# Column-tiled level products and paired heads in the chunked recurrence of a two-block model

## The chip, the core and the metric

The kernel runs on one core of a Trainium2 chip. TensorE (PE) multiplies, VectorE (DVE), ScalarE (ACT) and GpSimd (POOL) work element by element, and SyncE (SP) issues the loads. The metric is device time in microseconds: 2993.26 us is the median of three runs of the kernel before (2992.8 to 2993.64).

## The reference, cut to what matters

The program computes two blocks of two layers each for 1024 tokens. The change lies in the first block, whose two layers hold a gated recurrence of 4 heads, each with 128 channels:

```python
diff = G[:, :, :, None, :] - G[:, :, None, :, :]
decay = jnp.exp(jnp.where(causal, diff, MASK_VALUE))
scores = jnp.einsum('bhtd,bhsd,bhtsd->bhts', qc, kc, decay)
o = (jnp.einsum('bhts,bhsv->bhtv', scores, vc)
     + jnp.einsum('bhtd,bhdv->bhtv', qc * jnp.exp(G), S))
```

The score of query t and key s is the product over the channels of q at t, k at s and every forget gate between the two. The output of each head is then normalised over its channels, multiplied by a gate and goes into an up projection.

## The kernel before, in words

**Stages.** The first block runs as layer 0 half 0, layer 0 half 1, layer 1 half 0 and layer 1 half 1; a half is 512 tokens, four blocks of 128 tokens side by side. Each half-layer is a list of units. A unit (`col_unit`) loads a weight slab, splits it into a high and a low part (`split_w`: the cast `wh` and the difference `wl`) and runs `unit`, 24 matmuls of 512 columns (L261 to L263; 12 in the up projections), whose rate sets the pace.

**Fibers.** Everything else is written as Python generators (fibers). Each `yield` ends a step, and after every 24 matmuls (`tick`, `TICK`) each live fiber is advanced by one step, so that its products stand between two units. `finish` runs fibers to their end at once. `Engine` keeps a running load, by which `copy` and `tt` choose between DVE, ACT and POOL. The instructions of each engine are in the order in which the framework's scheduler then puts them, and each engine works its queue in that order.

**The recurrence.** `hgrn_half` is one fiber for one head and one half. It builds the scores by doubling the distance b between neighbours. After every level the second members of the pairs of q are multiplied on DVE by the gates (L791), the first members of k on POOL (L794), in place, and the gate products `tot` are shortened. The scores of the level are the product of k and q, of which a mask lets through what belongs to that level:

- b = 1 (L741): 8 products of 64 keys with 128 columns, written to PSUM rows 0 to 63 and 64 to 127 in turn (column tiles);
- b = 2, 4, 8, 16 (`level`, L725): 4 products of 128 keys with 128 queries, and one `copy_predicated` of 128 rows by 512;
- b = 32 (L770) and b = 64 (L783): 8 products of 32 by 32 (two column tiles in turn) and 4 of 64 by 64 (one column tile).

Each of these products is in f32 and shows in the trace as two passes, two LDWEIGHTS and two MATMUL. Then come the transpose of k (L806), the states (L813), the output (L838, L842), its squares, their mean (L397 with `ones_h`), the reciprocal root (`rstd_of`: a Sqrt on ACT, then a RECIPROCAL and three SCALAR_TENSOR_TENSOR on DVE) and the last two steps: a scaling of the output by it on DVE (L851) and the product with the gate (L854).

**Order of the heads.** `head(hd)` appends three units (forget gate, query, output gate). When the third is done, `gwork` spawns the head's fiber. Units of `gates_a` stand between the heads, so before the change the four fibers start 3, 6, and 6 units apart and overlap. `bsplit` waits for all four (`finish(st["hf"])`) after the sixth `gate_h` unit and splits their results; two units and a half later `up_h` of column 0 is the first to read them. The softmax attention (L636 to L713) runs as fibers of its own beside all that; its L703 and L709 are column-tiled too.

## Time and profile before

| | |
|---|---|
| median of 3 runs | 2993.26 us |
| profiled execution, time | 2993.03 us |
| its span | 2991.1 us |
| granted TensorE clock, mean | 0.992 |
| PE, DVE, ACT, POOL busy | 98%, 56%, 49%, 37% |

PE is busy all along, and the chain of work that ended last lies on PE for 92% of the span. A row of the timeline gives the start, the length, the engine, the line, the operation and the tiles; matmuls overlap in their pipeline, so what one costs is read from the start of it to the start of the next, not from its length.

### The profile page before, as it was taken

What the parts mean: (1) busy time and instruction counts of PE and PEld (TensorE: products, weight loads), DVE (VectorE), ACT (ScalarE), POOL (GpSimd) and SP (SyncE); (2) the same over time, 40 slices, a digit from 0 to 9 for tenths busy, and PEclk for the clock granted to TensorE, in tenths of its full rate; (3) what the DMA queues carried; (4) which work ended last, traced back from release to release, by engine and by line L of the source; (5) the groups of instructions that cost most, each with busy time, mean ns of one, the idle gap of its engine ahead of it and who ended that gap; (6) DMA issues with size and microseconds to landing.
All of it is one profiled execution on the core that took longest, in us unless ns stands there. A gap on an engine that the chain in (4) does not pass through costs nothing.

```text
span 2991.1 us, 43769 instructions
## 1 busy us (share of the span) xinstructions
PE 2927.6 (98%) x16204; PEld 2431.8 (81%) x16204; DVE 1683.4 (56%) x3322; ACT 1455.9 (49%) x2946; POOL 1098.8 (37%) x1182
## 2 busy tenths in 40 slices
PE   7999999999999999999999999999999899999997
PEld 7787887888878888788888888888888788878777
DVE  6657745556556566766666533435334644454456
ACT  5765326742357433574334455335544645564553
POOL 3545433543435433545332333213332322232332
PEclk9999999999999999999999999999999999999999
DMA  3212242122521224312243222533234111111123
GB/s 129 71 64 95 88 148 85 64 71 91 170 85 68 74 80 160 106 64 78 74 152 131 99 96 95 176 102 124 99 110 165 57 38 61 38 61 43 64 99 113
DMA packets 101493, 283.47 MB, mean 95 GB/s; under 512 B 11288, under 2 KB 15512, under 8 KB 101280
## 3 DMA queue, kind: packets, MB, share of 16 engines
q1 hardware_dynamic: 100016, 279.51, 27.6%
q8 instruction: 128, 2.10, 0.3%
q10 hardware_dynamic: 1264, 1.17, 0.1%
q14 instruction: 85, 0.70, 0.1%
HBM read 259.66 MB, written 20.97 MB: 94 GB/s over the span
## 4 chain that ended last, share of the span: by engine, by line
PE 92%; DVE 3%; issue 2%; POOL 1%; ACT 1%; DMA 1%; DVEq 0%; SPq 0%; POOLq 0%; ACTq 0%
PE mm L261 21%; PE mm L262 21%; PE mm L263 21%; PE mm L305 3%; PE mm L304 3%; PE mm L303 3%; DVE hp L76 2%; PE aux L725 2%; PE aux L1500 2%; PE aux L1546 2%; PE aux L1536 2%; PE mm L275 1%; PE mm L277 1%; PE mm L276 1%; PE aux L656 1%
## 5 line engine op out<-in xcount | busy, mean ns | idle before, releaser
L261 PE MATMUL mm<-hp,wh 128*128 128x512 f32 (+1 forms) x2816 | 1117.8, 397 | 0.0
L262 PE MATMUL mm<-hp,wh 128*128 128x512 f32 (+1 forms) x2816 | 1093.4, 388 | 1.8 <-POOL hp L76 1.8
L263 PE MATMUL mm<-hp,wl 128*128 128x512 f32 (+1 forms) x2816 | 1093.2, 388 | 0.0
L76 POOL TENSOR_TENSOR wl<-raw,wh 128x512 fp32r<-128x512 f32 x367 | 493.0, 1345 | 788.5 <-ACT wh L76 677.7
L76 ACT CAST wh<-raw 128x512 fp32r<-128x512 f32 x581 | 358.5, 620 | 681.7 <-PE mm L262 467.2
L76 POOL TENSOR_TENSOR hp<-hp,hp 128x256 f32<-128x256 f32 (+3 forms) x353 | 387.6, 1105 | 672.0 <-DVE hp L76 236.3
L261 PEld LDWEIGHTS mm<-hp,wh 128*128 128x128 f32 x2816 | 530.1, 188 | 115.3 <-issue 11.5
L263 PEld LDWEIGHTS mm<-hp,wl 128*128 128x128 f32 x2816 | 529.7, 188 | 109.9 <-issue 0.2
L262 PEld LDWEIGHTS mm<-hp,wh 128*128 128x128 f32 x2816 | 530.5, 188 | 104.3 <-POOL hp L76 3.1
L76 DVE TENSOR_TENSOR wl<-raw,wh 128x512 fp32r<-128x512 f32 x449 | 360.8, 806 | 214.2 <-ACT wh L76 174.1
L76 DVE TENSOR_TENSOR hp<-hp,hp 128x512 f32<-128x512 f32 (+3 forms) x401 | 289.6, 731 | 149.8 <-ACT hp L76 103.0
L76 ACT ACT_TABLE_LOAD x247 | 316.9, 1283 | 23.8 <-PE mm L263 10.5
L76 DVE TENSOR_TENSOR hp<-mm,hp 128x512 f32<-128x512 f32 (+2 forms) x264 | 166.4, 636 | 157.5 <-ACT hp L76 78.0
L76 ACT ACTIVATE hp<-mm 128x512 f32<-128x512 f32 (+2 forms) x296 | 168.3, 579 | 156.2 <-PE mm L305 74.6
L76 ACT CAST hp<-hp 128x512 fp32r<-128x512 f32 (+1 forms) x207 | 116.0, 573 | 217.6 <-POOL hp L76 182.2
L76 DVE CAST wh<-raw 128x512 fp32r<-128x512 f32 x235 | 120.8, 515 | 179.5 <-PE mm L262 147.0
L303 PE MATMUL mm<-wh,hp 128*128 128x512 f32 x480 | 187.8, 391 | 0.0
L76 POOL TENSOR_SCALAR sP<-sP,a2l 128x640 f32<-128x640 f32 (+4 forms) x128 | 88.0, 689 | 271.4 <-DVE a2l L76 147.4
L304 PE MATMUL mm<-wl,hp 128*128 128x512 f32 x480 | 187.1, 390 | 0.0
L305 PE MATMUL mm<-wh,hp 128*128 128x512 f32 x480 | 187.0, 390 | 0.0
L76 ACT ACTIVATE sP<-sP,a2nm 128x640 f32<-128x640 f32 (+4 forms) x128 | 88.3, 691 | 96.4 <-DVE a2nm L76 96.3
L275 PE MATMUL mm<-wh,hp 128*128 128x256 f32 x384 | 114.6, 298 | 13.6 <-DVE hp L76 10.6
(203 smaller groups left out, 3452.7 us busy)
## 6 DMA issues: line engine op xcount, KB each, us to landing
raw<-in_w_ch_dram SPq DMA_DIRECT2D x128, 512.0 KB, 3.2
raw<-in_g_uz_dram SPq DMA_DIRECT2D x64, 512.0 KB, 3.2
hp<-xd SPq DMA_DIRECT2D x88, 256.0 KB, 4.1
raw<-in_w_up_dram SPq DMA_DIRECT2D x64, 256.0 KB, 2.6
raw<-in_w_o_dram SPq DMA_DIRECT2D x32, 512.0 KB, 3.2
raw<-in_g_v_dram SPq DMA_DIRECT2D x32, 512.0 KB, 4.1
raw<-in_g_o_dram SPq DMA_DIRECT2D x32, 512.0 KB, 3.7
raw<-in_w_wide_dram SPq DMA_DIRECT2D x28, 512.0 KB, 4.0
```

What stands on the lines that cost most here:

```text
L76: self.last = f(*args, **kw)
L261: nc.tensor.matmul(ps, wh[:, c : c + P], rh, start=(k == 0), stop=False)
L262: nc.tensor.matmul(ps, wh[:, c : c + P], rl, start=False, stop=False)
L263: nc.tensor.matmul(ps, wl[:, c : c + P], rh, start=False, stop=(k == nk - 1))
L275: nc.tensor.matmul(ps, lh[:, o : o + P], wh[:, c : c + n], start=(k == 0), stop=False)
L303: nc.tensor.matmul(ps, lh[:, s], wh, start=(k == 0), stop=False)
L304: nc.tensor.matmul(ps, lh[:, s], wl, start=False, stop=False)
L305: nc.tensor.matmul(ps, ll[:, s], wh, start=False, stop=(k == KD - 1))
L725: nc.tensor.matmul(ps[:, s], k[:, s], q[:, s], start=True, stop=True)
L1500: nc.tensor.matmul(ps[:, 0:w], lhs[r, o : o + P], rhs[r, k0 : k0 + w], start=(j == 0), stop=(j == 2))
L1536: nc.tensor.transpose(ps[:, j * P : (j + 1) * P], S[:, (i + j) * P : (i + j + 1) * P], self.ident)
L1546: nc.tensor.matmul(po[e * 64 : e * 64 + 64, 0:P], vv, pts[e][:, i * P : (i + 1) * P], start=(i == 0), stop=(i == nb - 1),)
```

## The change

Two edits. In `level` the four products of 128 keys with 128 queries become eight of 64 keys with 64 queries, written to the two column tiles in turn, since for b up to 16 no pair crosses a border of 64 tokens; the `copy_predicated` becomes two, one for each half of the rows. And the fibers of heads 0 and 1, and of heads 2 and 3, are handed to a new generator, `together`, which is spawned when the second of the two is ready and advances both by one step at a time.

```diff
+    def together(self, fs):
+
+        fs = list(fs)
+        while fs:
+            for f in list(fs):
+                if next(f, self) is self:
+                    fs.remove(f)
+            if fs:
+                yield
...
             ps = self.aux()
-            for c in range(4):
-                s = slice(c * P, (c + 1) * P)
-                nc.tensor.matmul(ps[:, s], k[:, s], q[:, s], start=True, stop=True)
-            nc.vector.copy_predicated(c4(SC), self.mask[:, msk, None, :].to_broadcast([P, 4, P]), c4(ps))
+
+            for i in range(8):
+                o = (i % 2) * 64
+                s = slice(i * 64, i * 64 + 64)
+                nc.tensor.matmul(ps[o : o + 64, s], k[:, s], q[:, s], start=True, stop=True)
+            for o in (0, 64):
+                d = slice(o, o + 64)
+                nc.vector.copy_predicated(
+                    c4(SC)[d, :, d], self.mask[d, msk, None, d].to_broadcast([64, 4, 64]), c4(ps)[d, :, d]
+                )
...
-            st["hf"].append(self.spawn(self.hgrn_half(st, l, hd, half, f, k, q, g)))
+            st["pair"].append(self.hgrn_half(st, l, hd, half, f, k, q, g))
+            if hd % 2:
+                st["hf"].append(self.spawn(self.together(st["pair"])))
+                st["pair"] = []
```

What stands on PE between two units in layer 0 half 0, before: head 1's states (L813) and one level of head 2 (L725). Names are tiles: `aux` is a PSUM bank, `hp` a buffer in SBUF, `wh` and `wl` the parts of a weight slab.

```order
L263 MATMUL mm469_2323<-hp188_977,wl439_2171 128x512
L813 MATMUL aux471_2352<-hp181_951,hp462_2302 128x128
L813 MATMUL aux471_2352<-hp194_994,hp462_2302 128x128
L813 MATMUL aux471_2352<-hp210_1089,hp462_2302 128x128
L813 MATMUL aux471_2352<-hp218_1131,hp462_2302 128x128
L725 MATMUL aux475_2364<-hp411_2047,hp391_1958 128x128 x4
L261 MATMUL mm481_2383<-hp165_869,wh452_2252 128x512
```

The same half after the change: a level of head 2 and the same level of head 3 (L737 is the product in `level` now).

```order
L263 MATMUL mm516_2601<-hp188_977,wl500_2483 128x512
L737 MATMUL aux518_2628<-hp408_2045,hp388_1946 64x64 x8
L737 MATMUL aux519_2642<-hp487_2450,hp469_2379 64x64 x8
L261 MATMUL mm533_2693<-hp165_869,wh512_2593 128x512
L262 MATMUL mm533_2693<-hp166_870,wh512_2593 128x512
```

The levels of two heads stand back to back. So do 28 of the 32 pairs of levels; in the other four one or more unit matmuls stand between the two. Over the program PE has 64 stretches of L703, L709, L741, L770 and L783 between instructions of the full width before, and 80 stretches of these and of `level` after.

The second place is DVE at the end of layer 0 half 1, from the reciprocal of head 3 on. Before:

```order
RECIPROCAL hp1384_6755<-hp1384_6755 128x512
CAST wh1417_6895<-raw1416_6893 128x512
SCALAR_TENSOR_TENSOR hp1385_6756<-aux1383_6752,eps_95,hp1384_6755 128x512
TENSOR_TENSOR wl1418_6896<-raw1416_6893,wh1417_6895 128x512
SCALAR_TENSOR_TENSOR hp1385_6756<-hp1385_6756,hp1384_6755 128x512
CAST wh1421_6915<-raw1420_6913 128x512
SCALAR_TENSOR_TENSOR hp1384_6755<-hp1385_6756,hp1384_6755 128x512
TENSOR_TENSOR wl1422_6916<-raw1420_6913,wh1421_6915 128x512
SCALAR_TENSOR_TENSOR hp1377_6717<-hp1377_6717,vec_97,hp1384_6755 128x512
```

This is one chain, with the weight parts of the next columns (`wh`, `wl`) between its links. After, heads 2 (`hp1381`, `hp1369`) and 3 (`hp1384`, `hp1374`):

```order
RECIPROCAL hp1381_6903<-hp1381_6903 128x512
CAST wh1417_7055<-raw1416_7053 128x512
SCALAR_TENSOR_TENSOR hp1382_6904<-aux1380_6900,eps_95,hp1381_6903 128x512
RECIPROCAL hp1384_6913<-hp1384_6913 128x512
SCALAR_TENSOR_TENSOR hp1382_6904<-hp1382_6904,hp1381_6903 128x512
SCALAR_TENSOR_TENSOR hp1385_6914<-aux1383_6910,eps_95,hp1384_6913 128x512
SCALAR_TENSOR_TENSOR hp1381_6903<-hp1382_6904,hp1381_6903 128x512
SCALAR_TENSOR_TENSOR hp1385_6914<-hp1385_6914,hp1384_6913 128x512
SCALAR_TENSOR_TENSOR hp1369_6848<-hp1369_6848,vec_97,hp1381_6903 128x512
SCALAR_TENSOR_TENSOR hp1384_6913<-hp1385_6914,hp1384_6913 128x512
TENSOR_TENSOR hp1401_6976<-hp1078_5267,hp1400_6975 128x512
SCALAR_TENSOR_TENSOR hp1374_6865<-hp1374_6865,vec_97,hp1384_6913 128x512
```

Head 2's reciprocal has moved from the middle of head 3's levels to this place, and the two weight slabs that stood inside the chain now follow it. From the end of the first block on, the order on every engine is that of the kernel before, and SP's is so throughout.

## Rows read from the trace of the kernel before

**Rows 1.** The page: the span, the busy time of the engines, and the chain that ended last by engine.

```profile
span 2991.1 us, 43769 instructions
PE 2927.6 (98%) x16204; PEld 2431.8 (81%) x16204; DVE 1683.4 (56%) x3322; ACT 1455.9 (49%) x2946; POOL 1098.8 (37%) x1182
PE 92%; DVE 3%; issue 2%; POOL 1%; ACT 1%; DMA 1%; DVEq 0%; SPq 0%; POOLq 0%; ACTq 0%
```

**Rows 2.** The waits of PE from 80 to 1580 us: who waited for whom, us in total, times, the longest; the first two of four rows.

```profile
PE aux L397 <- DVE hp L76: 8.4, 5, 4.7
PE aux L684 <- POOL hp L76: 3.8, 3, 1.7
...
```

**Rows 3.** The chain that ended last, from 214 us: start, us, what, and how many instructions; below it the timeline of PE at 230 us (start, us, what).

```profile
216.41 0.89 PE aux L725 x8
217.30 0.23 PE mm L261
...
231.01 1.05 PE L725 MATMUL aux<-hp,hp 128*128 128x128 f32 x8
231.82 0.48 PE L261 MATMUL mm<-hp,wh 128*128 128x512 f32 x1
```

**Rows 4.** The timeline of PE and of its weight loads (PEld): a level of b = 32 alone between two units, one of b = 64 alone, one of b = 1, and one of `level`.

```profile
237.13 0.39 PE L263 MATMUL mm<-hp,wl 128*128 128x512 f32 x1
237.44 0.33 PEld L770 LDWEIGHTS aux<-hp,hp 128*32 128x32 f32 x16 [0.35 <-issue]
237.82 0.50 PE L261 MATMUL mm<-hp,wh 128*128 128x512 f32 x1
...
285.79 0.39 PE L263 MATMUL mm<-hp,wl 128*128 128x512 f32 x1
286.11 0.54 PEld L783 LDWEIGHTS aux<-hp,hp 128*64 128x64 f32 x8 [0.35 <-issue]
286.71 0.50 PE L261 MATMUL mm<-hp,wh 128*128 128x512 f32 x1
...
126.42 0.85 PEld L741 LDWEIGHTS aux<-hp,hp 128*64 128x64 f32 x16
```

**Rows 5.** What one line's weight loads took: count, then ns at least, median and most.

```profile
L770 PEld LDWEIGHTS aux<-hp,hp x256: 106/113/114, 166.2 to 1438.2; 128*32 128x32 f32 x128
L783 PEld LDWEIGHTS aux<-hp,hp x128: 132/138/138, 174.5 to 1444.4; 128*64 128x64 f32 x128
L741 PEld LDWEIGHTS aux<-hp,hp x256: 132/137/138, 126.4 to 1403.2; 128*64 128x64 f32 x128
```

**Rows 6.** Groups of instructions on DVE and ACT, shapes apart (the last from the page): count, busy us, mean ns of one, idle time before.

```profile
L76 DVE COPY_PREDICATED hp<-mask,aux 128x512 f32<-128x512 uint8 x64 | 47.4, 740 | 59.0 <-PE aux L725 58.9
L76 DVE COPY_PREDICATED hp<-mask,aux 64x256 f32<-64x256 uint8 x32 | 14.3, 446 | 0.9
L76 DVE RECIPROCAL hp<-hp 128x512 f32<-128x512 f32 x26 | 87.1, 3349 | 19.9 <-ACT hp L76 19.7
L76 ACT ACT_TABLE_LOAD x247 | 316.9, 1283 | 23.8 <-PE mm L263 10.5
```

**Rows 7.** Layer 0 half 0, the wait in the middle of head 3: timeline of DVE, POOL, ACT and PE, and then two windows (length, busy us of PE, PEld, DVE, ACT, POOL with counts, granted clock, DMA).

```profile
280.81 3.34 DVE L76 RECIPROCAL hp<-hp 128x512 f32<-128x512 f32 x1
288.17 3.92 POOL L76 TENSOR_TENSOR hp<-hp,hp 128x512 f32<-128x512 f32 x2 [0.20 <-DVE hp L76]
290.87 0.62 ACT L76 CAST hp<-hp 128x512 fp32r<-128x512 f32 x1 [3.16 <-POOL hp L76]
292.04 0.69 DVE L76 TENSOR_TENSOR wl<-raw,wh 128x512 fp32r<-128x512 f32 x1 [2.35 <-ACT wh L76]
297.63 0.76 PE L397 MATMUL aux<-hp,ones_d 128*128 128x512 f32 x1 [4.73 <-DVE hp L76]
...
292.00:298.00 6.00, 1.27 (x7) 0.93 (x7) 5.65 (x5) 4.46 (x8) 5.20 (x4) 0.94 0.07 29
298.00:305.00 7.00, 7.00 (x26) 5.58 (x26) 4.99 (x4) 1.36 (x3) 1.29 (x1) 0.81 0.33 112
```

**Rows 8.** The ends of layer 0 half 0 (above) and of layer 0 half 1 (below): DVE's reciprocal of head 3, the scaling of the output, the last splits, and the matmuls of `up_h` that read them.

```profile
323.32 3.35 DVE L76 RECIPROCAL hp<-hp 128x512 f32<-128x512 f32 x1 [1.54 <-ACT hp L76]
330.26 1.78 DVE L76 SCALAR_TENSOR_TENSOR hp<-hp,vec,hp 128x512 f32<-128x512 f32 x1
332.12 7.69 POOL L76 TENSOR_TENSOR hp<-hp,hp 128x512 f32<-128x512 f32 x5 [0.63 <-DVE hp L76]
340.28 1.28 DVE L76 TENSOR_TENSOR hp<-hp,hp 128x512 fp32r<-128x512 f32 x2
342.53 0.39 PE L262 MATMUL mm<-hp,wh 128*128 128x512 f32 x1
...
706.92 3.35 DVE L76 RECIPROCAL hp<-hp 128x512 f32<-128x512 f32 x1 [1.59 <-ACT hp L76]
715.79 3.55 POOL L76 TENSOR_TENSOR hp<-hp,hp 128x512 f32<-128x512 f32 x1 [2.83 <-DVE hp L76]
720.08 1.30 POOL L76 TENSOR_TENSOR hp<-hp,hp 128x512 fp32r<-128x512 f32 x1 [0.74 <-ACT hp L76]
725.89 0.39 PE L262 MATMUL mm<-hp,wh 128*128 128x512 f32 x1
```

More of the change, by code (lines that the diff above doesn't have):

```diff
@@ L861, in layer_a @@
               "b32": [None] * 4, "o": [None] * 4, "V": [None] * 4, "carry": carry,
-              "kvf": [], "wait": FWAIT if first else 0, "qf": [], "hf": [], "rs": None, "rs8": None, "norm": []}
+              "kvf": [], "wait": FWAIT if first else 0, "qf": [], "hf": [], "rs": None, "rs8": None, "norm": [], "pair": []}
         ht = h
```

## The prediction

> **What bounds the kernel now.** I read the page first: PE is busy for 98% of the span, and the chain that ended last lies on PE for 92% of it [rows 1]. So an instruction taken from PE comes off the end, and work on DVE, ACT or POOL counts only where PE waits for it. The waits of PE in the first block, where the whole change lies, come next: none is for a level's operands, and the longest row is the mean of squares (L397), 8.4 us in five waits [rows 2]. The levels stand in the chain with their full time [rows 3].
>
> **The levels, before.** From the start of a level that follows another f32 product to the start of the next unit matmul 0.89 us pass (216.41 to 217.30), 0.81 us where an fp32r product stands ahead (231.01 to 231.82) [rows 3]. There are four levels in each of 16 head-halves, 64 in all (the count of the 128-row `copy_predicated` [rows 6]). With 0.87 as the mean, since 9 of them stand behind an fp32r product and 4 behind a unit by the order and the rest behind f32 ones: 64 x 0.87 = 55.7 us.
>
> **The levels, after.** A level is 8 products of 64 keys by 64 queries, 16 passes. No row shows just this form with the two column tiles in turn. The nearest rows bound it. The spacing of passes is (length less one load) / (count less 1). For b = 64, the same 64 by 64 form but on one column tile: (0.54 - 0.138) / 7 = 57.4 ns. For b = 32, 32 by 32 on two tiles in turn: (0.33 - 0.113) / 15 = 14.5 ns. For b = 1, 64 keys by 128 columns on two tiles in turn: (0.85 - 0.137) / 15 = 47.5 ns [rows 4, 5]. So 14.5 ns from below and 57.4 from above. A straight line by columns between b = 32 and b = 1 gives 14.5 + 33.0 / 3 = 25.5 ns at 64 columns; two tiles that work wholly side by side, each at the pace of b = 64, give 57.4 / 2 = 28.7. I take 28.7, from the row of the same form. 1024 passes then take 29.4 us.
>
> To this comes the change between the full width and column tiles. The lone level of b = 32 takes 237.82 - 237.13 = 0.69 us of the stream, of which the unit matmul ahead has 0.23 and its 16 passes 16 x 14.5 ns = 0.23: 0.23 are left. For b = 64, 286.71 - 285.79 = 0.92, less 0.23, less 8 x 57.4 ns = 0.46: 0.23 again [rows 4]. Each column-tiled stretch pays this once. The order shows 64 such stretches before and 80 after, although 64 levels have joined them, because two heads' levels, and their b = 1, b = 32 and b = 64, stand together: 16 x 0.23 = 3.7 us. **Sum on PE: 29.4 + 3.7 - 55.7 = -22.6 us.**
>
> **What the other engines pay.** Each level has two `copy_predicated` of 64 rows, 0.446 us each, where it had one of 0.740 [rows 6]: 64 x (0.892 - 0.740) = 9.7 us more on DVE, which has 44% of the span free [rows 1]. The order has 20 ACT_TABLE_LOAD fewer, 20 x 1.283 = 25.7 us less on ACT [rows 6], because two Sqrt now follow one load. Both lie beside PE's units and cost or give nothing by themselves. What the pairing adds is a possible wait: a step of one head on DVE is now queued in front of the same step of the other. As PE comes to the level one step (24 matmuls of 0.23 us, 5.4 us) later, two heads' copies and gate products must fit in it, and two heads overlapped for most of the time before too, without a wait [rows 2]. I take 0 here; if the cover is gone, each level waits for about one more DVE step, 0.892 us plus a gate product of about the same, and 32 of those would be 57 us. Nothing in the rows is near that.
>
> **The moved reciprocal.** Head 2's normalisation moves from the middle of head 3's levels to the end, beside head 3's own. At two places this counts.
>
> First, layer 0 half 0, the wait of 4.73 us before L397 at 297.63. It is the end of a queue that begins with head 2's reciprocal at 280.81 on DVE: POOL's product waits for the chain behind it, ACT's cast for POOL (3.16 us), DVE's weight part for ACT (2.35 us), and the sums that L397 reads come behind that [rows 7]. After the wait the granted clock is 0.81 over 7 us, against 1.00 around it: another 7 x 0.19 = 1.3 us. In the new order that reciprocal isn't there. Between 0 and 6.0 us come back; I take 4, since the same DVE also gets head 2's level steps there.
>
> Second, the end of each half-layer. Before, one chain runs from the reciprocal on, and PE reads the results in `up_h`. In layer 0 half 1 the reciprocal starts at 706.92, POOL's last difference ends at 720.08 + 1.30 = 721.38, and PE reads it at 725.89: 4.5 us to spare. In layer 0 half 0, where the second half's first normalisation runs as well, DVE's last difference ends at 341.56 and the two are read from 342.53 on, which leaves 1 us or so [rows 8]. After, the order puts two reciprocals (3.35 each [rows 6]), eight SCALAR_TENSOR_TENSOR (0.68 to 0.74, without a disturbance), a cast (0.36) and a difference (0.67) up to the second scaling: 6.7 + 5.7 + 1.0 = 13.4 us, where the chain before ended when POOL's product could start, at 715.79, after 8.9 us. In layer 0 half 1 this gives 706.9 + 13.4 = 720.3; then POOL's product (1.45), ACT's cast (0.62) and DVE's difference (0.68): 723.1, still 2.8 us before PE's read. Not all is undisturbed: the POOL product at 715.79 took 3.55 us, so up to 2.1 us more may come, and on DVE the single operations beside POOL at 330.26 took 1.78 in place of 0.74 [rows 8]. I take 0.5 us of waiting for each of the three later halves, 1.5 in all. In layer 0 half 0 the 4.5 us that come on top of the chain (13.4 - 8.9) meet 1 us to spare: a wait of some 3 us and a lower clock behind it for 1 us, 4 in all. What is late next there are the weight parts that now stand behind the chain; they are read right after `up_h` of column 0.
>
> Together -4 + 4 + 1.5 = +1.5 us. Bounds: -6.0 + 0 + 0 from below; from above 0 and four ends at the full extra DVE work of 6.2 us (one reciprocal and four of 0.71) with 1.3 us of lower clock, 4 x 7.5 = 30 us.
>
> **The sum.** The profiled execution took 2993.03 us (span 2991.1), 0.2 us from the median, so no correction is made: 2993.0 - 22.6 + 1.5 = 2971.9, **2972 us**.
>
> **A rule that speaks against it.** At b = 32 and b = 1 loads and products of the two tiles overlap: the passes follow at 14.5 and 47.5 ns, although one weight load is shown with 113 and 137 ns [rows 4, 5]. The Trainium skill, page "TensorE: Matmul & The Clock Gate", section "The mechanism" in Part 3, says that a weight load overlaps with running matmuls only where the two use different row groups. The two column tiles here use the same rows, so by that rule the loads of a pair of passes would stand one after the other and only the products run together. It is a rival below.
>
> **Rivals.**
>
> 1. *The weight loads of the two tiles take turns.* A pass at b = 64 would be half load and half product (57.4 / 2 = 28.7 each, as both have 64 columns), and a pair two loads and one product: 86 ns, 43 a pass. 1024 x (43 - 28.7) = 14.6 us more: 2986.6 us. Against it: b = 32 at 14.5 ns a pass is a quarter of b = 64's on half the columns, so nearly all of it runs side by side; for it, that b = 1 at 47.5 ns lies well above a half of what one tile would need [rows 4, 5]. By the page's rule it would be this one. Chance 0.10.
>
> 2. *The ends of the half-layers turn into waits, and it is slower.* The place is `up_h` of column 0, which reads the split of heads 2 and 3; the price is up to 7.5 us for each half-layer, 30 in all, and 2993.0 - 22.6 + 30 = 3000 us, 7 us slower. It decides where the two chains with their disturbances last longer than the 4.5 us to spare and the 4.5 that they add. For it: DVE at 5.65 us busy of 6 around 295 [rows 7], and operations of 1.78 for 0.74. Against it: 2.8 us still to spare in the undisturbed sum. Chance 0.10.
>
> 3. *The two tiles don't run side by side at all,* 57.4 ns a pass: 1024 x 28.7 ns = 29.4 us more, 3001 us. Against it stand b = 32 and b = 1, both below 57.4 at the same or double the columns [rows 4]. Chance 0.05.
>
> 4. *The pairing doesn't bring the levels together on the chip,* each pays its own 0.23: 32 x 0.23 = 7.4 us more, 2979 us. The order speaks against it with 28 of 32. Chance 0.05.
>
> **How the numbers follow.** The forecast has 0.70. Its own range is 2963 to 2981: 25.5 ns in place of 28.7 and the whole wait of half 0 given back are 5.3 us below, the upper end has some 9 us of waits at the ends. The range for 8 in 10 reaches on to rival 1 and to half of rival 2: 2962 to 2989. What this kernel's measurement can tell from no change is about 0.2%, 6 us. Faster by more than that: the forecast, rivals 1 and 4, which hold 0.85 together, less 0.05 for a forecast that is spoiled by waits: 0.80. Slower: rival 3 and most of rival 2, 0.11. Within 0.2%: what is left, 0.09.
>
> **What would show it.** Right: on the chain a pair of levels with about 1.1 to 1.2 us where one level had 0.89; the passes of the level at 25 to 30 ns; no wait of PE for a level's operands; the wait of L397 near 297 us short or gone. Wrong: passes at 43 or 57 ns (rivals 1, 3); PE waiting for POOL or DVE at L261 and L262 near the ends, with a granted clock below 1 behind it (rival 2); unit matmuls between the two heads' levels (rival 4).

## The result, and the profile after

The changed kernel takes 3023.4 us (median of 4 runs, 3021.6 to 3029.29) where the kernel before takes 2993.45 (median of 4). The ratio is 1.0101, with a 95% interval of 1.0089 to 1.0113: it is 30 us slower, and 2972 us were forecast, with a range up to 2989. The profiled execution took 3021.6 us.

The page after, where [rows 1] stood before: the span, the busy times, the chain that ended last.

```profile
span 3019.8 us, 44834 instructions
PE 2926.3 (97%) x16716; PEld 2413.3 (80%) x16716; DVE 1734.5 (57%) x3391; ACT 1421.8 (47%) x2921; POOL 1094.9 (36%) x1182
PE 84%; DVE 5%; POOL 4%; issue 3%; ACT 2%; DMA 1%; SPq 0%; DVEq 0%; POOLq 0%; ACTq 0%
```

PE's share of the chain has fallen from 92% to 84%, and DVE and POOL have taken most of the difference. The busy time of PE is the same as before, although it has less to do: a busy PE is also one whose matmuls are stretched by a low clock.

The waits of PE from 80 to 1600 us after the change (who waited for whom, us in total, times, the longest), for [rows 2]:

```profile
PE mm L261 <- ACT hp L76: 10.3, 3, 3.5
PE aux L737 <- DVE hp L76: 9.0, 5, 2.9
PE mm L262 <- POOL hp L76: 7.1, 4, 5.2
PE aux L694 <- POOL hp L76: 5.9, 6, 1.7
PE aux L407 <- DVE hp L76: 5.1, 5, 2.0
PE mm L261 <- DVE hp L76: 1.9, 7, 0.4
PE aux L407 <- POOL hp L76: 1.6, 1, 1.6
PE aux L786 <- DVE hp L76: 1.4, 1, 1.4
```

These are the first eight of twelve rows. All twelve add up to 45.0 us, where those of before add up to 14.9 in the same window. L261 and L262 (the unit matmuls) and L737 (the level) had no wait in this stretch before. The unit matmuls that follow each other without a wait have lost another 10 us to a lower granted clock (their spacing above 0.227 us adds up to 23.2 us in the first block, 12.9 before). Without its waits, the time of PE between unit matmuls adds up to 198.2 us in the four recurrences, where it was 216.8 before: 18.6 us less.

**The level itself.** PE (first and third row) and its weight loads (second row), a pair of levels in layer 0 half 1:

```profile
656.14 1.15 PE L737 MATMUL aux<-hp,hp 128*64 128x64 f32 x32
656.14 1.01 PEld L737 LDWEIGHTS aux<-hp,hp 128*64 128x64 f32 x32 [0.35 <-issue]
657.23 0.50 PE L261 MATMUL mm<-hp,wh 128*128 128x512 f32 x1
```

The 32 passes follow at (1.01 - 0.138) / 31 = 28 ns. The unit matmul ahead starts at 655.83, so from it to the next unit 1.40 us pass, of which the unit has 0.23: a pair of levels costs 1.17 us. In the trace of single instructions the passes come in twos: the two loads of a two start 6 or 7 ns apart, one for each column tile, and a two follows some 58 ns after the last, which is the pace of one column tile alone (57.4 ns) [rows 4].

**Where the time went.** Both kernels have 8640 unit matmuls, and the k-th in one answers to the k-th in the other. Their starts, read from both traces, give the table: each cell is how much longer a stretch lasts than in the kernel before, in us (negative: shorter), by the profiled execution of each run. "Recurrence" is a half-layer up to 48 unit matmuls (two units) ahead of its up projections; "end" goes on from there to the 96th of the output projection, in layer 0 half 0 to the sixth column of the up projections, and the rest of that half has the row below it. Stretches that are left out differ by 2.3 us or less. e1 to e16 are the experiments below.

| stretch | after | e1 | e2 | e3 | e4 | e5 | e6 | e7 | e9 | e13 | e15 |
|---|---|---|---|---|---|---|---|---|---|---|---|
| l0 h0 recurrence | 3.5 | -3.0 | 2.7 | -12.8 | -4.1 | 1.0 | 1.3 | 3.9 | 3.7 | -4.1 | -3.4 |
| l0 h0 end | 8.6 | 0.2 | 8.5 | 7.8 | 2.6 | 0.0 | 1.8 | 7.2 | 8.0 | 9.5 | 1.8 |
| output, start of h1 | 0.0 | 1.1 | 0.1 | 7.7 | 1.1 | 5.5 | 5.2 | 0.0 | 0.0 | 0.0 | 0.0 |
| l0 h1 recurrence | -2.6 | -1.4 | -0.9 | -1.6 | -2.1 | 0.0 | 0.0 | -2.6 | -2.6 | -4.3 | -4.2 |
| l0 h1 end | 8.3 | 0.0 | 7.5 | 0.0 | 0.0 | 3.9 | 7.5 | 5.8 | 0.6 | 1.1 | 0.0 |
| l1 h0 recurrence | -3.4 | -1.6 | -0.8 | -2.3 | -2.2 | 0.0 | 0.0 | -1.7 | -3.3 | -5.0 | -5.0 |
| l1 h0 end | 8.5 | 0.0 | 8.4 | 0.0 | 0.0 | 2.4 | 4.1 | 6.8 | 0.6 | 0.0 | 0.0 |
| start of l1 h1 | 1.2 | 3.6 | 3.7 | -0.6 | 4.2 | 3.7 | 1.2 | 4.7 | -0.5 | -0.7 | 3.8 |
| l1 h1 recurrence | -3.3 | -1.4 | -0.8 | -2.4 | -2.1 | 0.0 | 0.0 | -3.3 | -3.4 | -5.0 | -5.0 |
| l1 h1 end | 7.4 | 0.0 | 8.2 | 0.0 | 0.0 | 3.9 | 7.4 | 5.6 | 0.6 | 0.0 | 0.0 |

The recurrence of the three later half-layers is 2.6 to 3.4 us shorter, as a cheaper level makes it. Each of the four ends is 7.4 to 8.6 us longer, 33 us in all. That is more than the whole loss. The start of layer 1 half 1 differs by some 4 us also in runs whose ends cost nothing (e1, e4); what moves it was not tried.

**A later end, seen close.** In the up projections each of eight columns needs 24 unit matmuls, 5.44 us, and leaves behind a chain: DVE multiplies PSUM with the gate, POOL adds, ACT casts the sum, DVE takes the difference. The output projection reads these pairs. One column in layer 0 half 1 after the change (POOL, DVE and ACT; start, us, what):

```profile
766.99 1.29 POOL L76 TENSOR_TENSOR wl<-raw,wh 128x512 fp32r<-128x512 f32 x1 [1.25 <-ACT wh L76]
767.04 1.53 DVE L76 CAST wh<-raw 128x512 fp32r<-128x512 f32 x1
769.69 0.68 DVE L76 TENSOR_TENSOR hp<-mm,hp 128x512 f32<-128x512 f32 x1
770.44 1.29 POOL L76 TENSOR_TENSOR hp<-hp,hp 128x512 f32<-128x512 f32 x1 [2.16 <-DVE hp L76]
771.76 0.62 ACT L76 CAST hp<-hp 128x512 fp32r<-128x512 f32 x1 [4.85 <-POOL hp L76]
772.29 0.62 ACT L76 CAST wh<-raw 128x512 fp32r<-128x512 f32 x1
772.42 0.69 DVE L76 TENSOR_TENSOR hp<-hp,hp 128x512 fp32r<-128x512 f32 x1 [2.05 <-ACT hp L76]
```

The same column in the kernel before:

```profile
752.61 0.42 DVE L76 CAST wh<-raw 128x512 fp32r<-128x512 f32 x1
753.52 0.62 ACT L76 CAST wh<-raw 128x512 fp32r<-128x512 f32 x1 [1.55 <-PE mm L262]
754.14 0.68 DVE L76 TENSOR_TENSOR hp<-mm,hp 128x512 f32<-128x512 f32 x1
754.22 1.29 POOL L76 TENSOR_TENSOR wl<-raw,wh 128x512 fp32r<-128x512 f32 x1 [2.91 <-ACT wh L76]
755.47 1.28 POOL L76 TENSOR_TENSOR hp<-hp,hp 128x512 f32<-128x512 f32 x1
756.79 0.62 ACT L76 CAST hp<-hp 128x512 fp32r<-128x512 f32 x1 [2.64 <-POOL hp L76]
757.44 0.69 DVE L76 TENSOR_TENSOR hp<-hp,hp 128x512 fp32r<-128x512 f32 x1 [2.61 <-ACT hp L76]
```

Before, ACT's cast `wh` waits for PE to free a slab (1.55 us), and so POOL's low part `wl` comes in the middle of the column. After, the chain is late and PE has freed the slab by then; ACT casts at once, POOL's `wl` starts at 766.99, just when DVE casts its own slab (767.04), and that cast takes 1.53 us in place of 0.42. As each engine works its queue in order, this closes a loop: difference, cast, product, POOL, ACT, difference. It takes 772.42 - 766.43 = 5.99 us after the change (the difference of the column before starts at 766.43) and 5.44 before (752.00 to 757.44), which is PE's pace. A late chain so becomes later with every column.

PE then stands at the first reader of the last column, in the output projection, and runs at a low clock behind it. The first two unit matmuls there, and windows of the same place (length, busy us of PE, PEld, DVE, ACT, POOL with counts, granted clock, DMA):

```profile
783.78 0.80 PE L261 MATMUL mm<-hp,wh 128*128 128x512 f32 x1 [3.47 <-ACT hp L76]
785.13 0.79 PE L262 MATMUL mm<-hp,wh 128*128 128x512 f32 x1 [0.55 <-POOL hp L76]
...
784.00:790.00 6.00, 5.45 (x13) 3.88 (x14) 1.29 (x2) 1.50 (x3) 2.30 (x2) 0.50 0.52 183
790.00:793.00 3.00, 3.00 (x15) 2.45 (x14) 1.50 (x2) 0.62 (x1) 1.56 (x1) 1.00 0.81 219
```

After 3.47 us without work the granted clock is 0.50 (of 2.4 GHz, so 1.2) for the next 6 us. Thirteen matmuls at 0.43 us in place of 0.227 are 2.6 us. With the waits of this end, 3.47 and 0.55 here and 0.20 and 0.35 in the columns ahead, that is 7.2 of its 8.3 us.

**Layer 0 half 0 is late in another place.** Its end, for the upper part of [rows 8]: DVE's two reciprocals, the second head's chain, its scaling, POOL's last products and differences, and PE's first read in `up_h`.

```profile
326.34 3.35 DVE L76 RECIPROCAL hp<-hp 128x512 f32<-128x512 f32 x1 [4.30 <-ACT hp L76]
330.81 3.35 DVE L76 RECIPROCAL hp<-hp 128x512 f32<-128x512 f32 x1
337.92 0.75 DVE L76 SCALAR_TENSOR_TENSOR hp<-aux,eps,hp 128x512 f32<-128x512 f32 x1 [3.22 <-PE mm L262]
344.62 1.78 DVE L76 SCALAR_TENSOR_TENSOR hp<-hp,vec,hp 128x512 f32<-128x512 f32 x1
346.48 6.13 POOL L76 TENSOR_TENSOR hp<-hp,hp 128x512 f32<-128x512 f32 x4 [0.63 <-DVE hp L76]
350.98 0.79 PE L262 MATMUL mm<-hp,wh 128*128 128x512 f32 x1 [5.17 <-POOL hp L76]
```

The read that had about 1 us to spare before now waits 5.17 us. DVE stands 3.22 us for a unit matmul (337.92). What it reads there does not come from a unit matmul, so the wait must be for the scratch tile that it writes, a buffer which PE still reads; e13, where this tile is another one, has no such wait.

**A level that waits.** Layer 0 half 1, DVE and PE; there is one such place in each later half-layer (1.74 to 1.75 us), and there are two in layer 0 half 0 (2.85 and 0.86):

```profile
654.47 4.08 DVE L76 TENSOR_TENSOR wl<-raw,wh 128x512 fp32r<-128x512 f32 x3
660.64 0.93 DVE L76 COPY_PREDICATED hp<-mask,aux 64x256 f32<-64x256 uint8 x2
663.07 2.11 DVE L76 TENSOR_TENSOR hp<-hp,hp 128x512 fp32r<-128x512 f32 x2 [1.50 <-ACT hp L76]
665.33 0.69 PE L737 MATMUL aux<-hp,hp 128*64 128x64 f32 x16 [1.75 <-DVE hp L76]
```

DVE has three low parts in front of the copies of the two heads, and then, in front of the second head's gate product (it is in the group at 663.07), a difference that itself waits 1.50 us for ACT.

### The profile page after: what moved, and what is told of

It reads as the page before. It is cut to its first block, busy times and chain, and to the rows that moved or that the text cites. A ratio compares the mean times of both kernels' runs of the same rounds, so it can differ in the third digit from the quotient of the medians.

```text
span 3019.8 us, 44834 instructions
## 1 busy us (share of the span) xinstructions
PE 2926.3 (97%) x16716; PEld 2413.3 (80%) x16716; DVE 1734.5 (57%) x3391; ACT 1421.8 (47%) x2921; POOL 1094.9 (36%) x1182
## 3 DMA queue, kind: packets, MB, share of 16 engines
q10 hardware_dynamic: 1264, 1.17, 0.1%
## 4 chain that ended last, share of the span: by engine, by line
PE 84%; DVE 5%; POOL 4%; issue 3%; ACT 2%; DMA 1%; SPq 0%; DVEq 0%; POOLq 0%; ACTq 0%
PE mm L261 19%; PE mm L262 19%; PE mm L263 18%; PE mm L305 3%; PE mm L304 3%; PE mm L303 3%; DVE hp L76 3%; POOL hp L76 2%; PE aux L1565 2%; PE aux L1519 2%; PE aux L1555 2%; ACT hp L76 1%; PE mm L275 1%; PE mm L277 1%; PE mm L276 1%
## 5 line engine op out<-in xcount | busy, mean ns | idle before, releaser
L261 PE MATMUL mm<-hp,wh 128*128 128x512 f32 (+1 forms) x2816 | 1122.2, 399 | 12.2 <-ACT hp L76 10.3
L262 PE MATMUL mm<-hp,wh 128*128 128x512 f32 (+1 forms) x2816 | 1098.6, 390 | 9.5 <-POOL hp L76 8.9
L76 POOL TENSOR_TENSOR wl<-raw,wh 128x512 fp32r<-128x512 f32 x356 | 477.8, 1345 | 837.8 <-ACT wh L76 670.5
L76 ACT CAST wh<-raw 128x512 fp32r<-128x512 f32 x568 | 349.8, 620 | 664.7 <-PE mm L262 452.3
L261 PEld LDWEIGHTS mm<-hp,wh 128*128 128x128 f32 x2816 | 532.4, 189 | 134.9 <-issue 13.9
L76 POOL TENSOR_TENSOR hp<-hp,hp 128x256 f32<-128x256 f32 (+3 forms) x364 | 398.7, 1106 | 639.9 <-DVE hp L76 298.5
L262 PEld LDWEIGHTS mm<-hp,wh 128*128 128x128 f32 x2816 | 532.7, 189 | 114.8 <-POOL hp L76 11.9
L76 DVE TENSOR_TENSOR hp<-hp,hp 128x256 f32<-128x256 f32 (+3 forms) x390 | 303.3, 789 | 109.8 <-ACT hp L76 90.3
L76 DVE CAST wh<-raw 128x512 fp32r<-128x512 f32 x248 | 145.4, 590 | 185.1 <-PE mm L262 145.1
L275 PE MATMUL mm<-wh,hp 128*128 128x256 f32 x384 | 115.2, 300 | 11.3 <-DVE hp L76 8.3
```

Of the source, the lines that this page charges most:

```text
L76: self.last = f(*args, **kw)
L261: nc.tensor.matmul(ps, wh[:, c : c + P], rh, start=(k == 0), stop=False)
L262: nc.tensor.matmul(ps, wh[:, c : c + P], rl, start=False, stop=False)
L275: nc.tensor.matmul(ps, lh[:, o : o + P], wh[:, c : c + n], start=(k == 0), stop=False)
```

## The experiments

Each run has its own runs of the kernel before beside it (2994.3 to 2995.4 us); ratios are against those.

**e1, the level alone, and e2, the pairing alone.** Each undoes one part of the change:

```diff
 e1
-            st["pair"].append(self.hgrn_half(st, l, hd, half, f, k, q, g))
-            if hd % 2:
-                st["hf"].append(self.spawn(self.together(st["pair"])))
-                st["pair"] = []
+            st["hf"].append(self.spawn(self.hgrn_half(st, l, hd, half, f, k, q, g)))
 e2
-            for i in range(8):
...
+            for c in range(4):
+                s = slice(c * P, (c + 1) * P)
+                nc.tensor.matmul(ps[:, s], k[:, s], q[:, s], start=True, stop=True)
+            nc.vector.copy_predicated(c4(SC), self.mask[:, msk, None, :].to_broadcast([P, 4, P]), c4(ps))
```

> The column-tiled level without the pairing: each head's fiber is spawned at its own output gate, as before the change. Theory A (the loss comes from the pairing, which puts two normalisations at the end of a half-layer and makes the up projections start late): a lone level has 16 passes of 28.7 ns and one change of form of 0.23 us, 0.69 us in place of 0.87, so 64 x 0.18 = 11.6 us come off the kernel before and nothing else changes: about 2981 to 2984 us. Theory B (the loss comes from the level itself, from the second copy_predicated on DVE or from its products): slower than before, up to 3020 us.

> The pairing without the column-tiled level: four products of 128 by 128 and one copy_predicated, as before the change. Theory A: the level's gain of some 23 us is missing and the loss of the pairing is all there, so above the changed kernel, 3030 to 3045 us. Theory B (the level is to blame): about 2990 us, as the merged stretches of b = 1, 32 and 64 save a few us.

Measured: e1 2990.96 us, ratio 0.9985 (0.9976 to 0.9995); e2 3030.0 us, ratio 1.0114 (1.0099 to 1.0129). The loss is the pairing's: theory B falls. The level alone gives 3.8 us, not 11.6. On PE it gives what was forecast, by another route: 48 of the 64 levels stand among full-width products and are only 0.10 us cheaper each (with the states ahead 1.60 us in place of 1.70), but 16 stand beside column-tiled products and are 0.45 cheaper, some 11.3 us in all. Waits take back 3.9 us in the recurrences (3.2 of them are new waits of the transpose, L822, for POOL in the later halves), and 1.1 and 3.6 are lost at the output of layer 0 half 0 and at the start of layer 1 half 1. Two full-width levels in a row cost 1.70 us in e2, so a pair that stands alone saves 0.53 in the changed kernel; with the pairs that have other products beside them (0.19 to 0.88) this is 4.4 to 4.5 us in each later half. In e2, paired but with one copy for each level, the levels wait 0.9 us for DVE in all, and in e1, with two copies but unpaired, not at all, where they wait 9.0 us in the changed kernel: these waits need both parts of the change.

**e3, e4 and e8: where the pairing costs.** e3 and e8 move head 3's units, e3 in the changed kernel and e8, its control, in the kernel before; e4 pairs heads 0 and 1 alone.

```diff
 e3, e8
         head(2)
-        gates_a(range(3, 6))
         head(3)
-        gates_a(range(6, 8))
+        gates_a(range(3, 8))
 e4
+            fiber = self.hgrn_half(st, l, hd, half, f, k, q, g)
+            if hd > 1:
+                st["hf"].append(self.spawn(fiber))
+                return
+            st["pair"].append(fiber)
```

> The changed kernel, with the three units of head 3 ahead of the gates 3 to 5 instead of behind them, so the pair of heads 2 and 3 starts and ends three units (some 16 us) earlier, and the two normalisations are done long before the up projections. Theory A1 (34 of the us lost lie at the four ends of the half-layers: the up projections and the wait at the first unit behind them): these go, about 2989 us, and no wait of PE above 1 us behind the up projections. Theory A2 (what costs is that a level waits for the copies of the twin head, all through the half-layer): the ends moved earlier change little, 3015 to 3023 us.

> The changed kernel with only heads 0 and 1 advanced together; heads 2 and 3 have fibers of their own, as before the change. Theory A1 (the ends): no end of a half-layer has two normalisations any more, so the 34 us go, and the levels of heads 2 and 3 pay their own change of form (28 of 0.23 us, 6.5): 2985 to 2996 us. Theory A2 (the levels wait for the twin): half of the loss stays, about 3005 us or more.

> A control for e3: the kernel before, without pairing and without the column-tiled level, with head 3's three units ahead of the gates 3 to 5. If the new place of head 3 gives or costs something by itself, it shows here; the kernel before had no waits at the ends of its half-layers to lose, so I expect 2990 to 2998 us, with the extra waits of layer 0 half 0 that e3 has (15 us) if they come from the new place, and without them if they come from the pairing.

Measured: e3 2993.25 us, ratio 0.9994 (0.9984 to 1.0003); e4 2989.81, 0.9982 (0.9972 to 0.9992); e8 3003.99, 1.0033 (1.0021 to 1.0045). In e3 and in e4 the three later ends cost 0.0 us, as the table shows; theory A1 holds and A2 falls for them. The first end still costs 7.8 us in e3. e8 came out above its forecast: the new place of head 3 costs by itself, 7.3 us at the output projection of layer 0 half 0, which e3 has too (7.7), and 0.8 to 1.0 in each later recurrence. Against this control the change gains 0.39% (1.0033 - 0.9994), some 11 us.

**e5 and e6: the kernel before, made late.** Nothing of the change is in these; the chain of head 3 is made longer.

```diff
         rstd = self.rstd_of(self.mean_bcast(sq, self.ones_h))
+        if hd == 3:
+            for _ in range(2):
+                nc.vector.reciprocal(rstd[:, 0:256], rstd[:, 0:256])
```

(e6: 0:512.)

> The kernel before, with two reciprocals more on 256 of the 512 columns of head 3's root (the second undoes the first): the end of each half-layer has 3.4 us more of DVE work in its chain. Theory C (the up projections are a loop DVE, POOL, ACT, DVE that does not catch up; the split of the last column has 0.45 us to spare before its reader, so lateness at the start comes out as a wait there, with the lower clock behind it): some 3 us of wait and up to 3 us of clock in each of the three later halves, and as much in the first: 3010 to 3018 us. Theory D (the prediction's: only the first read of the heads' results counts, with 4.5 us to spare): nothing in the three later halves, a few us in the first: 2994 to 3000 us.

> The same on all 512 columns: 6.7 us more at the end of each half-layer. Theory C: 6 us of wait and 3 of clock in each half-layer, 3024 to 3034 us. Theory D: 2.2 us of wait with some clock in each of the three later halves and 6 to 9 in the first: 3010 to 3016 us.

Measured: e5 3012.17 us, ratio 1.006 (1.0045 to 1.0075); e6 3022.43, 1.0096 (1.0081 to 1.0111). e6 lies 2 us below the range of theory C and 6 above that of theory D. In e5 theory D falls: 3.5 us more work in the chain, less than the 4.5 us that the first read had to spare, cost 3.9, 2.4 and 3.9 us at the later ends. In e5 the last four of DVE's casts in each later end stand beside a low part of POOL, but only one of them, which starts 0.04 to 0.05 us after POOL, is slowed; the other three start 0.01 to 0.02 us before POOL and are not (in layer 0 half 0 four casts are slowed). In layer 0 half 1 the slowed one is the middle one of these, with POOL's parts starting at 755.82, 761.15 and 767.19:

```profile
755.80 0.42 DVE L76 CAST wh<-raw 128x512 fp32r<-128x512 f32 x1
761.19 1.53 DVE L76 CAST wh<-raw 128x512 fp32r<-128x512 f32 x1
767.18 0.42 DVE L76 CAST wh<-raw 128x512 fp32r<-128x512 f32 x1
```

**e7: the changed kernel, made less late.** The three refining steps of the root are left out for heads 2 and 3.

```diff
+        if not refine:
+            return r
         nc.vector.scalar_tensor_tensor(out=t, in0=ps, scalar=self.eps, in1=r, op0=ALU.add, op1=ALU.mult)
```

> The changed kernel, leaving out the three refining steps of the reciprocal root for heads 2 and 3 (their output is a little less exact): 6 DVE instructions of 0.63 to 0.75 us, 4 us or more, less at the end of each half-layer. Theory C: the lateness of 2.8 us at the start of the up projections is gone, so the three later ends (7.4 to 8.5 us each) go wholly or nearly and the first becomes shorter by 4 us or more: 2993 to 3002 us. Theory D, or a loss that comes from something else than the length of the chain (buffers of two heads, the clock alone): 3012 us or more.

Measured: 3019.36 us, ratio 1.0079 (1.0062 to 1.0096). A miss: the later ends still cost 5.6 to 6.8 us. With 4 us less work the first column's difference comes only 1.2 to 2.0 us earlier (11.2, 12.1 and 10.8 us after the start of the up projections; 12.8, 13.3 and 12.8 in the changed kernel; 8.9 before), for the weight slabs that had queued up on DVE stand in front of it as well. That is still late enough: the last four columns have casts of 1.52 or 1.53 us. The length of the head's chain alone is not the cause. e6 tells lateness and collision apart: in all three later ends the first column's difference comes 13.5 us after the start, but in layer 1 half 0 none of the last casts meets POOL's low part (all take 0.42 us), and that end costs 4.1 us; in the other two three casts of 1.52 or 1.53 us do, and they cost 7.5 and 7.4.

**e9 and e10: the loop without its collision.** All casts of the up projections' slabs go to ACT, all their low parts to DVE; e10 is the kernel before with the same.

```diff
+        up = ("scalar", "vector")
...
-            col_unit(a["w_up"][l, 8 + j], 512, st["b"], lambda ps, j=j: up_h(j, ps))
+            col_unit(a["w_up"][l, 8 + j], 512, st["b"], lambda ps, j=j: up_h(j, ps), up)
```

> The changed kernel, with all casts of the up projections' weight slabs on ACT and all their low parts on DVE; before, the program's running load sent about half of them to DVE and POOL. Theory E (in the three later halves the loss is a loop that locks into a slower beat: when the up projections start late, POOL's low part falls on DVE's cast, which then takes 1.53 us in place of 0.42, and a column takes 6.0 us where PE needs 5.44): without a cast on DVE and a low part on POOL there is nothing to fall together, the columns keep PE's 5.44 us, and of the 24 us at the three later ends 15 or more come back: 2998 to 3009 us. Theory F (the loss is only the lateness of the first column, the slower beat is its effect): the ends stay at 6 to 8 us each, 3017 to 3024 us.

> A control for e9: the kernel before with the same engines for the up projections' slabs. It has no wait at these ends, so 2990 to 2997 us, unless the new engines cost something by themselves.

Measured: e9 2999.86 us, ratio 1.0019 (1.0009 to 1.0029), and each later end costs 0.6 us in place of 7.4 to 8.5; e10 2992.98, 0.9995 (0.9986 to 1.0005). Theory E's number holds: 23.5 us come back, and nothing is gained where there was no lateness. Its reasoning was not quite right. In the last four columns DVE still casts slabs and POOL still makes low parts, those of the output projection. What changed is the pace of the first columns, whose differences now start 4.93 us apart, where they were 5.6 apart before the change and after:

```profile
747.01 0.69 DVE L76 TENSOR_TENSOR hp<-hp,hp 128x512 fp32r<-128x512 f32 x1 [1.84 <-ACT hp L76]
751.94 0.69 DVE L76 TENSOR_TENSOR hp<-hp,hp 128x512 fp32r<-128x512 f32 x1 [1.84 <-ACT hp L76]
756.87 0.69 DVE L76 TENSOR_TENSOR hp<-hp,hp 128x512 fp32r<-128x512 f32 x1 [1.84 <-ACT hp L76]
```

The loop is now faster than PE's 5.44 us, catches up what it was late, and when the output projection's slabs come it is back on PE's pace, where the two do not meet. Its first differences come 11.4 to 12.1 us after the start, about as late as in e7, whose ends cost 5.6 to 6.8 us.

**e14: do the twin head's copies make the levels wait?**

```diff
-            for o in (0, 64):
+            for o in (0,):
```

> e9, leaving out the second copy_predicated of each level (the scores of keys 64 to 127 of a block lack those levels): 64 DVE instructions of 0.446 us less. Theory I (the waits of PE for a level's operands, 9 us, come from the twin head's copies and gate products in DVE's queue): the waits of the level's line fall to 5 us or less, and the time is 4 to 8 us below e9: 2992 to 2996 us. Theory J (they come from other work in DVE's queue, a burst of small instructions in layer 0 half 0 and, in the later halves, a low part that itself waits for ACT): the waits stay at 7 us or more, and the time within 3 us of e9.

Measured: 2988.64 us, ratio 0.9984 (0.9974 to 0.9993), 11 us below e9. No level waits for DVE any more; what is left of that line's waits in the first block is

```profile
PE aux L737 <- POOL hp L76: 1.4, 3, 0.5
```

The number goes with theory I, and by more than it gave. Theory J named rightly what else stood in the queue; a queue that is 0.446 us a level shorter gets past it in time.

**Versions meant to beat both: e11, e12, e13 and e15, with the control e16.** e11 is e4's pairing in layer 0 half 0 and e3's order with both pairs in the others; e12 is e9 with heads 2 and 3 unpaired in layer 0 half 0; e13 is e9 with scratch tiles of the root in dead buffers; e15 is e12 and e13 together; e16 is the kernel before with both additions of e13.

```diff
 e13
-        r, t = self.heap()[:, :n], self.heap()[:, :n]
+        r, t = rt or (self.heap()[:, :n], self.heap()[:, :n])
...
-        sq = self.split_pair(sq)
+        raw, sq = sq, self.split_pair(sq)
...
-        rstd = self.rstd_of(self.mean_bcast(sq, self.ones_h))
+        rstd = self.rstd_of(self.mean_bcast(sq, self.ones_h), rt=(kT, raw))
```

> A version meant to beat both: the column-tiled level everywhere; in layer 0 half 0 only heads 0 and 1 are paired and the units keep their order (as in e4), in the three later halves both pairs are formed and head 3 comes ahead of the gates 3 to 5 (as in e3). From the stretches of those two runs: about 0 for layer 0 half 0, -1.6, -2.3 and -2.4 us for the later halves and no loss at their ends: 2985 to 2990 us. If halves depend on what comes before them (the clock, the slabs' engines), it comes out at the 2990 to 2993 us of e3 and e4.

> A version meant to beat both: e9 (column-tiled level, paired heads, the up projections' casts on ACT and low parts on DVE), but in layer 0 half 0 heads 2 and 3 have fibers of their own as in e4. From the stretches of e9 and e4: -4 + 2.6 + 1.1 us for layer 0 half 0, -2.6, -3.3 and -3.3 for the later halves and +0.6 for each of their ends, 0 to 4 us between the last two halves: 2984 to 2990 us. If e9's gain at the ends depends on the lateness that the first half brings along, 2993 us or more.

> e9, with the two scratch tiles of a head's reciprocal root placed in buffers of the same head that are dead by then (the transposed keys and the squares), so that the root needs no buffer that PE still reads. Theory G (in layer 0 half 0 the second head's chain stands 3.2 us for a buffer that a unit still reads, and with it the wait of 5.2 us in front of the up projections): 3 to 5 us less than e9 in that stretch, 2994 to 2997 us. Theory H (the stretch is set by the sheer work of DVE and POOL there, the two normalisations beside that of the second half): same as e9 within 1 us in that stretch.

> e13 with heads 2 and 3 on fibers of their own in layer 0 half 0, as in e12. If the gains add (e12's first half: -4 and no loss at its end; e13's later halves: -4.3, -5.0 and -5.0 with +1.1 at one end), about 16 us below the kernel before: 2976 to 2982 us. If e13's gain hangs on the order that its first half brings along, 2984 to 2990 us.

> A control: the kernel before (no pairing, levels of 128 by 128) with both additions of e13, the up projections' engines and the root's scratch tiles in dead buffers. If these additions are what makes e13 fast, this comes to 2985 us or less; if they only take away what the pairing brought in, it stays at 2989 to 2996 us.

| run | us | ratio, 95% interval |
|---|---|---|
| e11 | 2988.77 | 0.9980 (0.9970 to 0.9989) |
| e12 | 2986.46 | 0.9974 (0.9965 to 0.9984) |
| e13 | 2986.15 | 0.9969 (0.9957 to 0.9981) |
| e15 | 2978.46 | 0.9943 (0.9929 to 0.9957) |
| e16 | 2989.50 | 0.9981 (0.9972 to 0.9991) |

e15 beats both kernels, by 17 us and 45 us, and the control e16 leaves 11 us of the 17 to the levels and the pairing as e15 has them. In e13 the stretch of theory G did not get shorter (9.5 us, e9 8.0), though its chain did: from the last mean of squares (L407) to the read in `up_h` it takes 24.2 us (321.45 to 345.67) where e9 needs 27.6 (323.93 to 351.55), 3.4 us more. In e9 DVE's wait for the buffer is only 0.98 us, though, where it was 3.22 in the changed kernel; another 1.79 us it waits for ACT ahead of the second reciprocal. Neither wait is there in e13. PE comes to that read earlier by more than the 3.4 us. The gain lies in the recurrence, where the waits of the levels for DVE fall from 8.9 to 1.3 us. The new buffers also changed the order of DVE's and POOL's queues; which of that did it was not tried and stays open.

## Why the prediction was wrong

**The levels on PE: right.** Passes at 28.7 ns were forecast and 28 measured, 1.15 us for a pair and 1.17 measured. The bound from below (14.5) and rivals 1 and 3 fall: the loads of the two tiles do not take turns, as they start 6 or 7 ns apart. For rival 1 the prediction drew on the Trainium skill, page "TensorE: Matmul & The Clock Gate", section "The mechanism" in Part 3, by which a weight load overlaps with running matmuls only where the row groups differ, and estimated 43 ns a pass. The trace disagrees with that estimate. Another page of the Trainium skill, "TensorEngine Tiling (Array Packing)", section "Key Properties", lets different tiles load and multiply in parallel. The trace agrees: two tiles together need 58 ns for two passes, one tile 57.4 for one. The sum of -22.6 us was somewhat too large all the same: 18.6 us were gained on PE, 4.9 to 5.0 in each later half, where 22.6 / 4 = 5.7 were forecast. One reason is that a pair saves 0.53 us (1.70 in e2, 1.17 now) and not 1.74 - 1.15 = 0.59. Where no level waits for DVE in the later halves (e13, e15) the later recurrences are 4.2 to 5.0 us shorter each by the table.

**The other engines' own work: right, and beside the point.** 160 - 32 = 128 copies at 0.445 us are 57.0 us where there were 47.4, 9.6 more (9.7 forecast), and 20 table loads fewer came as forecast:

```profile
L76 DVE COPY_PREDICATED hp<-mask,aux 64x256 f32<-64x256 uint8 x160 | 71.3, 445 | 18.6 <-PE aux L737 14.8
L76 ACT ACT_TABLE_LOAD x227 | 291.2, 1283 | 18.1 <-DVE a2nm L76 5.7 <-PE mm L263 4.7 <-PE aux L1278 1.4
```

**"I take 0 here": wrong.** The step that let two heads' copies fit into 5.4 us argued from a kernel whose twin heads were three units apart. The levels wait 9.0 us for DVE (and L786 1.4), at five places; e2 shows that with one copy for each level they hardly wait, and e14 that a shorter queue takes it away, worth 11 us with all that follows from it.

**The moved reciprocal, first place: right in size.** The wait of L407 near 297 us is 2.0 us where it was 4.7 [rows 7]; -2.7 us, with -4 forecast and 0 to -6 as bounds.

**The moved reciprocal, second place, is the step that failed.** It took 0.5 us for each later end and 4 for the first; measured are 8.3, 8.5 and 7.4, and 8.6. The sum went as far as the first reader, `up_h` of column 0, and stopped because 2.8 us were left there. In the later halves that was even true, with 1.3 us left (layer 0 half 1 after the change, the last difference on DVE and the read on PE):

```profile
733.72 0.69 DVE L76 TENSOR_TENSOR hp<-hp,hp 128x512 fp32r<-128x512 f32 x1
735.74 0.39 PE L262 MATMUL mm<-hp,wh 128*128 128x512 f32 x1
```

But lateness is not spent by a reader that can bear it. It stays in DVE's queue, in the slabs behind the chain and then in the loop of the up projections, whose last column in the kernel before had 0.45 us to spare (POOL's difference ends at 768.96, PE reads at 769.41). e5 shows it on the kernel before, without any of the change; e9 shows that a loop with reserve absorbs lateness of that size. On top of it the loop has two beats, 5.44 us and 5.99, and a late start can put it into the slower one (e6: 7.5 and 7.4 us with it, 4.1 without).

**Rival 2** had the right kind of event and a fair price (up to 7.5 us an end, 3000 us in all), and got 0.10; its place was wrong for three of four ends. That its 30 us lie so near the measured 33 is luck, since they were counted from DVE's extra work and not from the loop. Its 30 us were set against a level gain of 22.6 us, where 18.6 came, and the waits of PE in the recurrences, which grew by 12 us, were not added: together most of the way from 3000 to 3023.

## What to carry to other kernels

A deadline that is met is no end of the argument: follow late work to the last reader of everything that queues behind it, and ask of every loop across engines whether its own period is shorter than that of the engine which paces it; one that runs at the same period does not catch up. When two fibers are brought into step, their ends come into step too, and the second one's end pays for both; stagger them or give the stage behind them reserve first. A saving on the busiest engine makes every chain beside it relatively later, so it is worth its full size only where those chains have room.

## What the runs showed of the hardware

DVE's f32 to fp32r cast of 128x512 takes 0.42 us alone and 1.53 beside a POOL TENSOR_TENSOR of 1.29, so it waits for about the whole of it, but only where POOL has started first: in e5, where the cast leads by 0.01 us, it takes 0.42 us and POOL's part 1.56. ACT's cast takes 0.62 us without POOL at work (772.29) and with it (323.19 after the change, POOL busy from 323.12 to 324.39). The Trainium skill, page "GPSIMD Engine Reference", section "8. Key points", says that GpSimd shares its SBUF interfaces with VectorE and that DVE instructions in a 2-port mode or with two SBUF inputs contend. The trace agrees for the scaling, which has two inputs in SBUF: 0.74 us alone (726.48) and 1.78 beside POOL (344.62). The cast has one input, and no run here shows in which mode it works. Not expected was that such a collision can keep itself alive, because the wait for a free slab, which had kept the two apart, disappears as soon as the chain is late.

A wait of 3.5 us on PE costs 2.6 us more behind it: the granted clock is 0.50 for 6 us (784 to 790), 13 matmuls at 0.43 us in place of 0.227.
